# A two-layer decoder trunk on one core: its SBUF buffers laid out anew, in two stacks from the bottom and the top of a partition

## The chip, the cores and the metric

The kernel runs on one core of one Trainium2 chip. The metric is device time in microseconds (us) of one execution; three timed runs of the kernel before stand below. PE is TensorE (PEld its weight loads), DVE is VectorE, ACT is ScalarE, POOL is GpSimd, SP is SyncE, which issues the loads. Every tile lies in SBUF on 128 partitions; an address here is a byte within a partition, 0 at the bottom, 229376 at the top. All tiles of the kernel start at addresses that are fixed when the program is built.

## The reference

x is [512 tokens, 1024]. Layer 0 mixes by sparse attention and pooling, layer 1 by a convolution module; each layer ends in a feed-forward part with 2816 hidden channels.

```python
def conformer_conv(h, w_pw1, b_pw1, w_dw, b_dw, ln_g, ln_b, w_pw2, b_pw2):
    a, gt = jnp.split(h @ w_pw1 + b_pw1, 2, axis=-1)
    z = a * jax.nn.sigmoid(gt)
    z = lax.conv_general_dilated(z, w_dw[:, None, :], ..., feature_group_count=D_MODEL) + b_dw   # causal, 31 taps
    z = jax.nn.silu(layernorm(z, ln_g, ln_b))
    return z @ w_pw2 + b_pw2

def swiglu(h, w_gate, w_up, w_down):
    return (jax.nn.silu(h @ w_gate) * (h @ w_up)) @ w_down

for layer in range(2):
    h = rmsnorm(x, mix_norm[layer])
    x = x + (nsa_pool_mixer(h, ...) if layer == 0 else conformer_conv(h, ...))
    h = rmsnorm(x, ffn_norm[layer])
    x = x + swiglu(h, ffn_w_gate[layer], ffn_w_up[layer], ffn_w_down[layer])
return rmsnorm(x, final_norm)
```

## The kernel before

Channels lie on partitions, tokens in columns: the residual is 8 tiles `x0` to `x7` of 128 x 512. A product is exact to float32 in three float32r passes: both operands are split into a high and a low part, and for each of the k-tiles of the contraction TensorE runs high x high, high x low and low x high into one bank (`mm3`). The stationary operand is the split weight (`wh`, `wl`), the moving operand, 512 columns of it, the split activation.

- **Weights** come in units of 128 x 1024 (512 KB). SP loads each into one of 3 buffers `raw`; ACT writes `wh` (a copy to float32r), DVE (for some units POOL) writes `wl` = `raw` - `wh`, 3 buffers of each.
- **Norm pairs.** The residual times a norm's gain, split, stands in a ring of 8 pairs, `xs...h` and `xs...l`: `xsm0` feeds the attention's projections, `xsf0` the feed-forward part of layer 0, `xsm1` the first pointwise product of the convolution (`pa`, `pg`). The same ring holds the inputs of the attention's output product `op` (`mp`, `mo`, all but the pair `mo0`) and the convolution's results `ys` (input of the second pointwise product `p`, in halves of 256 tokens). The norm pairs of layer 1's feed-forward part, `xsf1`, stand in a ring of their own (pool `n1`, tags `xnh`, `xnl`).
- **Feed-forward part.** 22 hidden tiles in chunks of 8, 8 and 6. For each hidden tile a gate product `g` and an up product `u`, 8 k-tiles x 3 passes = 24 matmuls of 512 columns each, whose moving operands are the norm pairs; the hidden tile goes through the scratch tile `a` into a pair `hd...h`, `hd...l`. After a chunk come 8 down products `d` of 8 (or 6) x 3 matmuls, whose moving operands are the `hd` pairs, and DVE adds each to `x`. The last chunk of layer 1 runs its down products in halves of 256 columns.
- **Convolution module.** Tiles 0 to 4 are convolved by DVE, ACT and POOL from `z0` to `z4` (ACT products of one tap go to POOL by a ring of 8 buffers `pr`), tiles 5 to 7 by TensorE (`tz`, from `zp` into `zo`). Squares for the LayerNorm's variance are the tiles `lsq`.

The order of instructions on each engine is written out by a small planner inside the kernel (`run_tasks`), with its own table of costs; addresses play no part in it. Tiles get their addresses from pools, which are stacked from the bottom of a partition or, with `side="right"`, from its top, in the order in which they are opened. A ring's buffers are laid out when its first tile is made.

```python
with tc.tile_pool(name="cn", bufs=1) as cn, tc.tile_pool(name="wp", bufs=1) as wp, \
        tc.tile_pool(name="xp", bufs=1) as xp, tc.tile_pool(name="ps", bufs=1, space=PSUM) as pp:
...
    raws[i] = wp.tile([P, UW], F32, name=f"raw{i}", tag="raw", bufs=3)
```

This is where the tiles that matter lie, from the program as built:

| tiles | read by TensorE as | bytes before | bytes after the change |
|---|---|---|---|
| DMA scratch | | 0 to 16384 | 0 to 1024 |
| `raw` (3) | | 19584 to 31872 | 208736 to 221024 |
| `wh`, `wl` (3 each) | stationary; moving in `pab`, `v` | 31872 to 56448 | 4224 to 28800 |
| `x0` to `x7` | | 56448 to 72832 | 192352 to 208736 |
| `xs` ring (8 pairs) | moving | 72832 to 89216, 91264 to 107648 | 28800 to 61568 |
| `acc`, `sq`, `bc` | | 89216 to 91264, 107648 to 113920 | 221024 to 229344 |
| `hd` pairs (both layers) | moving | 120064 to 152832 | 61568 to 94336 |
| `a` (3) | | 113920 to 120064 | 94336 to 100480 |
| `xsf1` | moving | 196576 to 229344 | in the `xs` ring |
| `ys` | moving | in the `xs` ring | 61568 to 94336 |
| `z0` to `z4` | | 113920 to 124800 | 94336 to 105216 |
| `pr` (8) | | 147712 to 164096 | 77952 to 94336 |
| attention's tiles | partly | 113920 to 228416 | 61568 to 176064 |

Of the kernel before, what the change touches and what calls it, by code (L numbers as in the profile page):

```python
# [7 lines left out]
F32 = mybir.dt.float32  # L8
# [5 lines left out]
P = 128  # L14
T = 512            # tokens
D = 1024           # model width
KT = D // P        # k-tiles of the model width
TB = T // P        # token blocks
NH = 8             # heads
DH = 64  # L20
NC = 31            # compressed blocks
FH = 2816
FT = FH // P       # 22 hidden tiles
FCH = (8, 8, 6)    # hidden tiles by chunk
CW = 31            # conv taps
UW = D             # widest weight unit (columns)
# [4 lines left out]
# columns of the packed constants (shapes only)  # L31
C_ID = 0           # identity
C_ONE = 128        # ones
C_HALF = 256       # -0.5 [4]
C_REP = 260        # identity of 32, repeated [4, 32]
C_ATT = 388        # from here on only for the attention layer
C_M = 0            # token distances, masked
C_MC = 512         # distances to compressed blocks, transposed: rows [2, 32], a column per token
C_CNT = 1024       # 1 / min(t + 1, w) [4, 16]
C_Q = 1088         # query scale by pair [4]  # L40
C_RM = 1092        # tokens with a whole compressed block [1]
C_SEL = 1093       # the blocks' two halves and their positions, summed [key / value, 2, 64]
NATT = 1349

# columns of the packed vectors
V_MN = 0           # mix_norm [2, 8]
V_FN = 16          # ffn_norm [2, 8]
V_FIN = 32         # final_norm [8]
V_PS = 40          # pool_scale [4]
V_BP1 = 44         # conv_b_pw1 [16]  # L50
V_DW = 60          # conv_w_dw [8, 31]
# [4 lines left out]
V_PK = 340         # cmp_pos_k [16]  # L56
V_PV = 356         # cmp_pos_v [16]
NVEC = 372

PH = 4             # token phases that TensorE's convolution puts on the partitions  # L60
NTZ = 37 * PH      # columns of a tile's taps and bias, by phase
# the plan: times are in microseconds of the engines' clocks that run_tasks keeps; a prio is a place in TensorE's work
WINDOW = 600       # tasks that are looked at
WB = 3             # buffers of split weights
BANKS = {'A': 2, 'B': 2, 'C': 2, 'D': 2}
AHEAD = 10.5       # how long before its product a weight unit's split becomes urgent
TOL = 0            # how late a more urgent task may be and still go first, in layer 0
TOL1 = 0.1         # and in layer 1
SHARE = (0, 40)    # weight units whose low parts VectorE and GpSimd share

# layer 0
FILL = (39, 55, 72, 88, 95, 105, 114)   # where queries and pool channels are projected
I0 = 50            # the first item: a head's branch
ITEM = 7.0         # from an item to the next
LAG = 17.0         # from an item's scores to its values
# [5 lines left out]
CEARLY = 4         # items from a head pair's compressed weights to its first item  # L81
# [4 lines left out]
PBRANCH = 9       # item that the pooling goes with  # L86
SBANK = 15         # items before the scores take turns in two rings of banks
LEAD0 = 3          # output projections that start with the first inputs

# layer 1  # L90
VT = 5             # conv tiles of the other engines
PRB = 8            # products on the way from ScalarE to GpSimd
SLACK = 0        # room that GpSimd's part of a conv tile leaves
TZLAG = 1          # tiles between a gate and TensorE's convolution
MEANS = 97         # where the first half's means are taken
LATE = (4, 7)      # tiles that come after the others' mean is taken
MARGIN = 2
HIGHS = (1, 3, 5)   # tiles of the first half whose high parts ScalarE may take
LEAD = 2           # second pointwise products that start with the first results
LATE1 = 20  # L100
LNB = 122          # where the second half's norm is
PREP2 = 17         # AHEAD of the second pointwise products
# [18 lines left out]
def body(tc, I, out):  # L121
# [17 lines left out]
    class Engine:  # L139
        """An engine: its instructions stay in their order, and are timed."""  # L140
# [5 lines left out]
        def about(self, n):  # L146
            """The time of an instruction on n columns, roughly."""
            return self.cost("", n, ())
# [4 lines left out]
        def __getattr__(self, name):  # L153
            def emit(*args, **kw):
# [3 lines left out]
                parts = tile_of(out)[:2] in ("zp", "zo", "tz")        # written by parts  # L158
# [17 lines left out]
    class Products(Engine):  # L176
        """The tensor engine, whose clock follows how busy it was in the tick before."""
# [51 lines left out]
    def hop(a, b):  # L229
        """From an engine's result to another's start."""  # L230
        return b.chain if a is b else HOPS.get((a, b), 0.06)
# [3 lines left out]
    def fetch(dst, src):  # L235
        """A load, timed."""
        nc.sync.dma_start(dst, src)
        loads[0] = max(loads[0], (used.get(tile_of(dst)) or (0.0,))[0] + 1.5) + cols(dst) * P * 4 / 360e3
        wrote[tile_of(dst)] = (loads[0] + 1.0, None)

# [1 line left out]
    queue, slots, fill_from, tol = [], {}, [0.0], [TOL]  # L242

    class Task:
        """A step on an engine, or on the soonest of several; end: when it ends, once it is emitted."""
# [24 lines left out]
    class Buf:  # L270
        """A tile of a ring of buffers, made by its first task; it waits for the uses of the one before it."""
# [17 lines left out]
    def put(engines, fn, deps=(), prio=0.0, n=T, new=(), into=(), uses=(), after=(), first=False):  # L289
        """A task that calls fn with its engine when deps have ended and after has begun; the lower prio first.  # L290
        new: buffers that it writes first; into: others that it writes; uses: those that it reads."""
# [12 lines left out]
    def resolve(t):  # L304
        """When a task can start, as far as its inputs go."""
# [12 lines left out]
    def candidate(e, open_tasks):  # L318
        """An engine's next task, and when it would start."""
# [49 lines left out]
    class Timed:  # L369
        """A pool whose tiles wait, in that timing, for the ones before them in their buffers."""  # L370
# [12 lines left out]
    class Stage:  # L383
        """A pool that is opened when it is first used, after others are closed."""
# [51 lines left out]
    with tc.tile_pool(name="cn", bufs=1) as cn, tc.tile_pool(name="wp", bufs=1) as wp, \  # L436
            tc.tile_pool(name="xp", bufs=1) as xp, tc.tile_pool(name="ps", bufs=1, space=PSUM) as pp:
        cn, wp, xp, pp = (Timed(v) for v in (cn, wp, xp, pp))
# [6 lines left out]
        n1 = Stage("n1", [tzs], side="right")  # L445
        f1 = Stage("f1", [cv])
# [13 lines left out]
        def load_to(n):  # L460
            while next_load[0] < min(n, len(units)):
                i = next_load[0]
                w = units[i].shape[1]
                raws[i] = wp.tile([P, UW], F32, name=f"raw{i}", tag="raw", bufs=3)
                fetch(raws[i][:, :w], units[i])
                next_load[0] += 1

        def unit_split(i, prio):
            """The task that ends the split of a weight unit into two float32r parts."""
# [32 lines left out]
        def product(tag, u, src, name, prio, deps=(), seg=ALL, by_k=None, lead=None, ahead=AHEAD, floor=-1e9):  # L502
            """A weight unit's product with src's pairs of buffers: its task, its bank.
            by_k: what the steps wait for; lead: the steps' own prio, to start with the first inputs."""
# [29 lines left out]
        class Norm:  # L534
            """The residual, scaled by a norm's gain and split; 1/rms by token."""

            def __init__(self, tag, gcol=None, pool=xp, ring="xs"):
# [4 lines left out]
                if gcol is not None:  # L542
                    self.hs = [tuple(Buf(pool, ring + p, KT, f"xs{tag}{j}{p}", dtype=F32R) for p in "hl") for j in range(KT)]
# [3 lines left out]
            def write(self, b):  # L547
                """How a task writes one of the norm's buffers: as the first, or after others."""
# [5 lines left out]
            def tile(self, j, seg, deps, prio, late=0.0):  # L554
                """Tasks for a tile of the residual: its parts, its squares added up."""
# [15 lines left out]
            def stats(self, seg, prio, tag="D"):  # L571
                """Tasks that bring 1/rms to all partitions."""
# [12 lines left out]
        def rsqrt(name, n, sp, sums, eps, prio, tag, shift=None):  # L585
            """Per token 1/sqrt(sums / D + eps), on all partitions in a bank: the task, the bank, the values by token block.
            shift: tasks, bank and place of other sums, whose squares / D are first taken off."""
# [27 lines left out]
        def residual(j, seg, t, o, prio, bias=None):  # L615
            """A product added to a tile of the residual."""
# [8 lines left out]
        def gate_up(l, c, fp, us, nm, hid, prio, lead=0):  # L625
            """Hidden tiles of a chunk, split."""
            for i in range(FCH[c]):
# [6 lines left out]
                k = put(V, lambda e, a=a, go=go: V.tensor_tensor(a(), go(), nm.bc(), op=ALU.mult), [g, *nm.done.values()], p + 5, new=(a,), uses=(go, nm.bc))  # L634
# [487 lines left out]
        def conformer(nm, base):  # L1122
# [26 lines left out]
            class Conv:  # L1149
# [9 lines left out]
                def src(self, k):  # L1159
                    return z[self.i][:, k:k + T]  # L1160
# [433 lines left out]
```

## Time and profile before

| | before |
|---|---|
| median of 3 runs | 1222.38 us (1222.06 to 1223.82) |
| span of the profiled execution | 1220.5 us |
| TensorE busy in the span | 1145.4 us (94%), 5563 matmuls |
| mean granted clock of TensorE | 0.973 |
| VectorE, ScalarE, GpSimd busy | 706.8, 506.2, 364.6 us |
| read from HBM | 106.66 MB, 89 GB/s over the span |

The profile gives the span from the first to the last instruction; the runs' times are those of whole executions, 1.9 us more at the median. A row of the timeline is an instruction with its start and its duration; the ends of matmuls are modelled, so the pace of TensorE is read from the starts, one product's start to the next one's. In the table of windows, "x" is the number of instructions in a stretch and PEclk the granted clock, 1.00 being 2.4 GHz.

### The profile page before, as it was taken

Reading aid. Unit: us, or ns where it says so; the run is one execution under the profiler, and the core shown is the slowest. Engines: PE = TensorE matmul, PEld = TensorE weight load, DVE = VectorE, ACT = ScalarE, POOL = GpSimd, SP = SyncE. Lnnn points to the kernel's source line nnn. Section 1 sums busy time; section 2 is a strip of 40 time slices with the busy share of each in tenths; the row PEclk is TensorE's granted clock in tenths of the full one; section 3 lists DMA queues with packets and bytes.
Section 4 is the critical chain, followed back from the end, with each engine's and each line's share of the span. In section 5 each row is a group of like instructions: output and inputs, shape, how many; then the busy total and the mean of one; then the engine's idle time right before and its main releaser. Section 6 shows DMA issues by size and latency. Waiting matters only on the chain. (4 is left out here: it accounts for less than half of the span.)

```text
span 1220.5 us, 14692 instructions
## 1 busy us (share of the span) xinstructions
PE 1145.4 (94%) x5563; PEld 952.1 (78%) x5563; DVE 706.8 (58%) x1064; ACT 506.2 (41%) x833; POOL 364.6 (30%) x317
## 2 busy tenths in 40 slices
PE   7989999999999999999999646899999999999996
PEld 5868878778888888888788536788888888888895
DVE  6778996556333433344589999695443333333355
ACT  5657685333222321223476446664332223222253
POOL 1056662166101110011269864242110011101123
PEclk9989999999999999999999877899999999999998
DMA  6311112223323232322322101144223232332243
GB/s 242 115 66 35 53 35 72 100 88 103 104 86 104 86 104 88 102 90 84 104 86 83 42 14 36 48 144 137 104 86 104 87 101 90 92 98 90 87 130 109
DMA packets 34264, 110.77 MB, mean 91 GB/s; under 512 B 3856, under 2 KB 6416, under 8 KB 34192
## 3 DMA queue, kind: packets, MB, share of 16 engines
q1 hardware_dynamic: 33904, 109.56, 28.0%
q8 instruction: 44, 0.72, 0.3%
q14 instruction: 28, 0.23, 0.1%
q10 hardware_dynamic: 288, 0.26, 0.1%
HBM read 106.66 MB, written 2.10 MB: 89 GB/s over the span
## 5 line engine op out<-in xcount | busy, mean ns | idle before, releaser
L155 ACT ACTIVATE wh<-raw 128x1024 fp32r<-128x1024 f32 (+4 forms) x205 | 209.2, 1025 | 532.5 <-PE d L155 161.9
L155 DVE TENSOR_TENSOR wl<-raw,wh 128x1024 fp32r<-128x1024 f32 (+3 forms) x193 | 240.4, 1248 | 35.9 <-ACT wh L155 32.5
L155 POOL TENSOR_TENSOR a<-a,bcf 128x512 f32<-128x512 f32 x44 | 78.4, 1783 | 541.1 <-ACT a L155 541.1
L155 POOL TENSOR_TENSOR cl<-cl,pr 128x512 f32<-128x512 f32 x69 | 99.4, 1443 | 48.2 <-ACT pr L155 43.5
L155 DVE TENSOR_TENSOR a<-u,a 128x512 f32<-128x512 f32 x44 | 30.4, 691 | 137.1 <-PE u L155 130.7
L155 DVE TENSOR_TENSOR x<-d,x 128x512 f32<-128x512 f32 (+1 forms) x56 | 34.3, 614 | 127.0 <-PE d L155 127.0
L155 DVE TENSOR_TENSOR a<-g,bcf 128x512 f32<-128x512 f32 x44 | 30.4, 691 | 122.4 <-PE g L155 115.9
L155 PE MATMUL tz<-zp,tz 128*128 128x128 f32 x216 | 32.0, 319 | 29.4 <-DVE zo L155 16.5
L155 PEld LDWEIGHTS tz<-zp,tz 128*128 128x128 f32 x216 | 31.3, 234 | 31.1 <-issue 19.8
L155 ACT ACTIVATE pr<-z,vec 128x512 f32<-128x512 f32 x69 | 46.7, 714 | 18.8 <-POOL cl L155 18.7
L155 DVE SCALAR_TENSOR_TENSOR cp<-z,vec,cp 128x512 f32<-128x512 f32 x75 | 54.0, 750 | 0.8
L155 POOL TENSOR_TENSOR p<-p,rc 128x512 f32<-128x512 f32 (+1 forms) x64 | 50.0, 802 | 2.4
L155 ACT ACTIVATE p<-s,mn 128x512 f32<-128x512 f32 (+1 forms) x64 | 33.3, 525 | 21.6 <-DVE mn L155 18.0
L155 DVE COPY zp<-ta 32x128 f32<-32x128 f32 x36 | 35.7, 992 | 0.6
L155 DVE CUSTOM_DVE_ANT_0 s<-s,att 128x512 f32<-128x512 f32 (+1 forms) x64 | 30.7, 503 | 8.4 <-PE s L155 8.2
L155 POOL TENSOR_TENSOR wl<-raw,wh 128x1024 fp32r<-128x1024 f32 (+1 forms) x12 | 29.5, 2469 | 17.4 <-ACT wh L155 17.3
L155 DVE TENSOR_TENSOR l<-tp,h 128x512 fp32r<-128x512 f32 (+1 forms) x48 | 27.9, 592 | 6.4 <-ACT h L155 6.2
L155 POOL TENSOR_TENSOR tz<-con,vph 128x1152 f32<-128x1152 f32 x12 | 30.0, 2526 | 0.0
L155 ACT ACTIVATE h<-tp 128x512 fp32r<-128x512 f32 (+1 forms) x48 | 24.4, 524 | 11.8 <-PE tp L155 11.1
L155 ACT ACTIVATE a<-a 128x512 f32<-128x512 f32 x44 | 27.2, 618 | 1.4 <-DVE a L155 1.3
L155 PE MATMUL s<-kh,qs 128*128 128x512 f32 (+1 forms) x64 | 21.7, 343 | 4.8 <-ACT p L155 4.8
L155 PE MATMUL tp<-con,p 128*128 128x128 f32 x160 | 24.0, 275 | 2.0 <-DVE l L155 2.0
(1326 smaller groups left out, 3425.1 us busy)
## 6 DMA issues: line engine op xcount, KB each, us to landing
raw<-in_w_gu SPq DMA_DIRECT2D x88, 512.0 KB, 3.5
raw<-in_w_dn SPq DMA_DIRECT2D x32, 512.0 KB, 3.5
raw<-in_w_p SPq DMA_DIRECT2D x32, 512.0 KB, 3.5
raw<-in_w_dn SPq DMA_DIRECT2D x24, 384.0 KB, 3.0
raw<-in_w_in SPq DMA_DIRECT2D x12, 512.0 KB, 4.0
raw<-in_w_out SPq DMA_DIRECT2D x8, 512.0 KB, 3.4
x<-in_x SPq DMA_DIRECT2D x8, 256.0 KB, 6.3
raw<-in_w_c SPq DMA_DIRECT2D x4, 512.0 KB, 3.8
```

Of the source, the lines that this page charges most:

```text
L155: tc.keep_in_program_order(getattr(self.eng, name)(*args, **kw))
```

## The change

Pools are opened in another order and on other sides. The split weights stand alone at the bottom, above them a new pool with the norm pairs; `raw`, `x`, `acc`, `sq` and `bc` move to the top. The ring of layer 1's own norm pairs goes, and `xsf1` takes the common ring. To make that free, the convolution's results `ys` get a ring `yh` and the ring `pr` in the convolution's pool, both made first; the squares of the second half's LayerNorm then take the rings `ta` and `tg` in place of `pr`. In the feed-forward pools the `hd` rings are made ahead of `a`. `zo` is made before `zp`, and the `z` tiles have 32 columns of padding ahead in place of 30. The scratch of the DMA queues shrinks. The comments and docstrings go too. Its code, but for those:

```diff
-    with tc.tile_pool(name="cn", bufs=1) as cn, tc.tile_pool(name="wp", bufs=1) as wp, \
-            tc.tile_pool(name="xp", bufs=1) as xp, tc.tile_pool(name="ps", bufs=1, space=PSUM) as pp:
+    with tc.tile_pool(name="cn", bufs=1) as cn, tc.tile_pool(name="wp", bufs=1) as wp, \
+            tc.tile_pool(name="xs", bufs=1) as xsp, tc.tile_pool(name="xp", bufs=1, side="right") as xp, \
+            tc.tile_pool(name="ps", bufs=1, space=PSUM) as pp:
...
-        n1 = Stage("n1", [tzs], side="right")
-        f1 = Stage("f1", [cv])
+        f1 = Stage("f1", [cv, tzs])
...
-                raws[i] = wp.tile([P, UW], F32, name=f"raw{i}", tag="raw", bufs=3)
+                raws[i] = xp.tile([P, UW], F32, name=f"raw{i}", tag="raw", bufs=3)
...
-                    self.hs = [tuple(Buf(pool, ring + p, KT, f"xs{tag}{j}{p}", dtype=F32R) for p in "hl") for j in range(KT)]
+                    self.hs = [tuple(Buf(xsp, "xs" + p, KT, f"xs{tag}{j}{p}", dtype=F32R) for p in "hl") for j in range(KT)]
...
+                def scaled(e, a=a, go=go, h=h, lo=lo, first=i == c == 0):
+                    if first:
+                        h(), lo()
+                    V.tensor_tensor(a(), go(), nm.bc(), op=ALU.mult)
...
+            yx = [(Buf(cv, "yh", KT, f"ys{i}h", dtype=F32R), Buf(cv, "pr", PRB, f"ys{i}l", dtype=F32R)) for i in range(KT)]
...
             def make_inputs(e):
+                for h, _ in yx:
+                    h()
+                G.memset(cv().tile([P, T], F32, name="pr", tag="pr", bufs=PRB)[:, 0:1], 0.0)
                 for i in range(KT):
                     if i < VT:
-                        z[i] = cv().tile([P, CW - 1 + T], F32, name=f"z{i}")
-                        G.memset(z[i][:, 0:CW - 1], 0.0)
+                        z[i] = cv().tile([P, ZP + T], F32, name=f"z{i}")
+                        G.memset(z[i][:, 0:ZP], 0.0)
...
-                    q = Buf(cv, "pr", PRB, f"lsq{hf}{i}") if hf else Buf(cv, "tg", 2, f"lsq{hf}{i}")
+                    q = Buf(cv, "ta", 1, "lsq10") if hf and not i else Buf(cv, "tg", 2, f"lsq{hf}{i}")
...
-                    if hf == 0:
-                        yx[i] = tuple(Buf(xp, "xs" + k, KT, f"ys{i}{k}", dtype=F32R) for k in "hl")
...
-            nm1 = Norm("f1", V_FN + KT, n1, "xn")
+            nm1 = Norm("f1", V_FN + KT)
...
-    nc = _bacc.Bacc("TRN2", target_bir_lowering=False, num_devices=1)
+    nc = _bacc.Bacc("TRN2", target_bir_lowering=False, num_devices=1, dynamic_dma_scratch_size=1024)
```

As built, PE, DVE, ACT and SP issue the same instructions in the same order as before; POOL issues one more. This is POOL's program at the start of the convolution module, of the kernel before; `z0` to `z4` are the padded inputs of the convolution.

```order
L155 TENSOR_TENSOR rm10_4987<-vm10_4985,con_67 128x4 [waits DVE_49]
L155 MEMSET z0_5017 128x30 [waits PE_49]
L155 MEMSET z1_5019 128x30
L155 MEMSET z2_5021 128x30
L155 MEMSET z3_5023 128x30
L155 MEMSET z4_5025 128x30
L155 MEMSET zp5_5027 128x4x8
```

And the same place after the change:

```order
L156 TENSOR_TENSOR rm10_4990<-vm10_4988,con_70 128x4 [waits DVE_49]
L156 MEMSET pr_5028 128x1 [waits PE_49]
L156 MEMSET z0_5030 128x32
L156 MEMSET z1_5032 128x32
L156 MEMSET z2_5034 128x32
L156 MEMSET z3_5036 128x32
L156 MEMSET z4_5038 128x32
L156 MEMSET zp5_5041 128x4x8
```

The added memset takes the first one's place and its wait for TensorE (the last down product of layer 0, whose `hd` tiles lay there). The second place is ACT's program at the LayerNorm of the second half of the tokens, where `lsq1i` is the square of tile i; before:

```order
L155 ACTIVATE lsq10_6243<-z0_5017 128x256 [waits DVE_49,Pool_49]
L155 ACTIVATE lsq11_6249<-z1_5019 128x256 [waits DVE_49,Pool_49]
L155 ACTIVATE lsq12_6255<-z2_5021 128x256 [waits DVE_49,Pool_49]
L155 ACTIVATE wh116_6262<-raw116_6064 128x1024 [waits DMAHW0_49,PE_49,Pool_49]
L155 ACTIVATE wh117_6276<-raw117_6091 128x1024 [waits DMAHW1_49,PE_49,Pool_49]
L155 ACTIVATE lsq13_6291<-z3_5023 128x256 [waits DVE_49]
L155 ACTIVATE lsq14_6296<-z4_5025 128x256 [waits DVE_49]
```

After:

```order
L156 ACTIVATE lsq10_6248<-z0_5030 128x256 [waits DVE_49]
L156 ACTIVATE lsq11_6254<-z1_5032 128x256 [waits DVE_49,PE_49]
L156 ACTIVATE lsq12_6260<-z2_5034 128x256 [waits DVE_49,PE_49]
L156 ACTIVATE wh116_6267<-raw116_6077 128x1024 [waits DMAHW0_49,PE_49,Pool_49]
L156 ACTIVATE wh117_6281<-raw117_6104 128x1024 [waits DMAHW1_49,PE_49,Pool_49]
L156 ACTIVATE lsq13_6296<-z3_5036 128x256 [waits DVE_49,Pool_49]
L156 ACTIVATE lsq14_6301<-z4_5038 128x256 [waits DVE_49,Pool_49]
```

The instructions stand as they stood. From `lsq13` on, each now waits until POOL has added the square two places before it, since its ring has two buffers in place of eight.

## Rows read from the trace of the kernel before

**Rows 1.** The page: busy time, share of the span and instructions of each engine.

```profile
PE 1145.4 (94%) x5563; PEld 952.1 (78%) x5563; DVE 706.8 (58%) x1064; ACT 506.2 (41%) x833; POOL 364.6 (30%) x317
```

**Rows 2.** The table of windows, all instructions; columns as in its first line.

```profile
core 0: us, PE busy (x) PEld busy (x) DVE busy (x) ACT busy (x) POOL busy (x), PEclk, DMA share, GB/s
400.00:500.00 100.00, 100.00 (x438) 81.79 (x437) 38.10 (x42) 24.98 (x29) 9.26 (x6) 1.00 0.31 96
700.00:800.00 100.00, 70.02 (x423) 63.97 (x423) 85.63 (x157) 56.45 (x105) 41.27 (x31) 0.80 0.14 45
1000.00:1100.00 100.00, 100.00 (x431) 80.72 (x430) 38.12 (x42) 25.03 (x29) 9.04 (x5) 1.00 0.30 95
```

**Rows 3.** The timeline of PE, layer 0: first matmul of a product g, u, d, g, u.

```profile
402.17 0.39 PE L155 MATMUL g<-xsf00h,wh 128*128 128x512 f32 x1
...
407.61 0.39 PE L155 MATMUL u<-xsf00h,wh 128*128 128x512 f32 x1
...
456.57 0.40 PE L155 MATMUL d<-hd010h,wh 128*128 128x512 f32 x1
...
501.36 0.39 PE L155 MATMUL g<-xsf00h,wh 128*128 128x512 f32 x1
...
506.81 0.39 PE L155 MATMUL u<-xsf00h,wh 128*128 128x512 f32 x1
```

**Rows 4.** The chain that ended last, in order of time: start, us, what, matmuls.

```profile
829.26 4.31 PE p L155 x36
...
912.83 5.60 PE g L155 x24
918.43 5.60 PE u L155 x24
924.03 44.62 PE d L155 x192
...
1058.25 44.62 PE d L155 x192
...
1172.41 17.94 PE d L155 x149
```

**Rows 5.** The timeline of PE in layer 1: matmuls of one up product.

```profile
918.50 0.39 PE L155 MATMUL u<-xsf10l,wh 128*128 128x512 f32 x1
918.73 0.40 PE L155 MATMUL u<-xsf10h,wl 128*128 128x512 f32 x1
918.97 0.39 PE L155 MATMUL u<-xsf11h,wh 128*128 128x512 f32 x1
919.20 0.39 PE L155 MATMUL u<-xsf11l,wh 128*128 128x512 f32 x1
```

**Rows 6.** The tile `raw` between 400 and 470: duration ns least/median/most, times.

```profile
L155 ACT ACTIVATE wh<-raw x13: 1061/1061/1064, 402.2 to 467.8; 128x1024 fp32r<-128x1024 f32 x13
L155 DVE TENSOR_TENSOR wl<-raw,wh x13: 1224/1225/1226, 403.3 to 468.9; 128x1024 fp32r<-128x1024 f32 x13
...
DMA to landing us min/median/max: 3.4/3.5/4.4
```

**Rows 7.** The timeline of PE, the attention's output product: first matmul of two products.

```profile
217.48 0.39 PE L155 MATMUL op<-mp0h,wh 128*128 128x512 f32 x1
...
222.97 0.39 PE L155 MATMUL op<-mp0h,wh 128*128 128x512 f32 x1
```

**Rows 8.** The timeline of POOL and of ACT, the second half's squares and the memsets.

```profile
606.70 0.35 POOL L155 MEMSET z<- 128x30 f32 x5
...
785.93 1.55 POOL L155 TENSOR_TENSOR lsq<-lsq,lsq 128x256 f32<-128x256 f32 x2 [3.35 <-ACT lsq L155]
788.89 4.28 POOL L155 TENSOR_TENSOR lsq<-lsq,lsq 128x256 f32<-128x256 f32 x3 [1.40 <-ACT lsq L155]
...
788.35 0.71 ACT L155 ACTIVATE lsq<-z 128x256 f32<-128x256 f32 x2
...
790.65 0.42 ACT L155 ACTIVATE lsq<-zo 128x256 f32<-128x256 f32 x1
```

**Rows 9.** The timeline of PE in the attention, moving operands from `wh` and `wl`.

```profile
39.60 0.28 PE L155 MATMUL pab<-wh,c2l 128*128 128x256 f32 x1
...
40.67 0.28 PE L155 MATMUL pab<-wh,c2l 128*128 128x256 f32 x1
...
48.86 0.29 PE L155 MATMUL v<-wh,xsm03h 128*128 128x280 f32 x1
48.99 0.30 PE L155 MATMUL v<-wl,xsm03h 128*128 128x280 f32 x1
...
49.65 0.29 PE L155 MATMUL v<-wh,xsm05h 128*128 128x280 f32 x1
49.78 0.29 PE L155 MATMUL v<-wl,xsm05h 128*128 128x280 f32 x1
```

More of the change, by code (lines that the diff above doesn't have):

```diff
@@ L58 @@
 NVEC = 372
+ZP = 32
 PH = 4
@@ L436, in body @@
     with tc.tile_pool(name="cn", bufs=1) as cn, tc.tile_pool(name="wp", bufs=1) as wp, \
-            tc.tile_pool(name="xp", bufs=1) as xp, tc.tile_pool(name="ps", bufs=1, space=PSUM) as pp:
-        cn, wp, xp, pp = (Timed(v) for v in (cn, wp, xp, pp))
+            tc.tile_pool(name="xs", bufs=1) as xsp, tc.tile_pool(name="xp", bufs=1, side="right") as xp, \
+            tc.tile_pool(name="ps", bufs=1, space=PSUM) as pp:
+        cn, wp, xsp, xp, pp = (Timed(v) for v in (cn, wp, xsp, xp, pp))
         at = Stage("at")
@@ L534, in body, with __init__ @@
         class Norm:
-            def __init__(self, tag, gcol=None, pool=xp, ring="xs"):
+            def __init__(self, tag, gcol=None):
                 self.tag, self.gcol = tag, gcol
@@ L633, in gate_up @@
                 g, go = product("A", us[i][0], nm.hs, "g" + t, p, lead=step)
-                k = put(V, lambda e, a=a, go=go: V.tensor_tensor(a(), go(), nm.bc(), op=ALU.mult), [g, *nm.done.values()], p + 5, new=(a,), uses=(go, nm.bc))
+                def scaled(e, a=a, go=go, h=h, lo=lo, first=i == c == 0):
+                    if first:
+                        h(), lo()
+                    V.tensor_tensor(a(), go(), nm.bc(), op=ALU.mult)
+                k = put(V, scaled, [g, *nm.done.values()], p + 5, new=(a,), uses=(go, nm.bc))
                 k = put(S, lambda e, a=a: S.activation(a(), a(), AF.Silu), [k], p + 5, uses=(a,))
@@ L1069, in pooled @@
                 uses_of[u_pool].append(t)
-                h, lo = mixed[i] = tuple(Buf(xp, "xs" + p, KT, f"mp{i}{p}", dtype=F32R) for p in "hl")
+                h, lo = mixed[i] = tuple(Buf(xsp, "xs" + p, KT, f"mp{i}{p}", dtype=F32R) for p in "hl")
                 sc = vec[:, V_PS + i:V_PS + i + 1]
@@ L1079, in head_out @@
                 if s == 0:
-                    mixed[4 + pr] = tuple(Buf(xp if pr else at, ("xs" if pr else "mo") + p, KT if pr else 1, f"mo{pr}{p}", dtype=F32R) for p in "hl")
+                    mixed[4 + pr] = tuple(Buf(xsp if pr else at, ("xs" if pr else "mo") + p, KT if pr else 1, f"mo{pr}{p}", dtype=F32R) for p in "hl")
                     outs[pr] = [Buf(ap, tag, 1, f"{tag}{pr}") for tag in ("om", "ol")], []
@@ L1134, in zc @@
             def zc(i, seg):
-                v = z[i][:, CW - 1:] if i < VT else zo[i]
+                v = z[i][:, ZP:] if i < VT else zo[i]
                 return v[:, seg]
             def make_inputs(e):
+                for h, _ in yx:
+                    h()
+                G.memset(cv().tile([P, T], F32, name="pr", tag="pr", bufs=PRB)[:, 0:1], 0.0)
                 for i in range(KT):
                     if i < VT:
-                        z[i] = cv().tile([P, CW - 1 + T], F32, name=f"z{i}")
-                        G.memset(z[i][:, 0:CW - 1], 0.0)
+                        z[i] = cv().tile([P, ZP + T], F32, name=f"z{i}")
+                        G.memset(z[i][:, 0:ZP], 0.0)
                     else:
+                        zo[i] = cv().tile([P, T], F32, name=f"zo{i}")
                         zp[i] = cv().tile([P, PH, 8 + T // PH], F32, name=f"zp{i}")
-                        zo[i] = cv().tile([P, T], F32, name=f"zo{i}")
                         G.memset(zp[i][:, :, 0:8], 0.0)
@@ L1159, in src @@
                 def src(self, k):
-                    return z[self.i][:, k:k + T]
+                    return z[self.i][:, ZP - CW + 1 + k:ZP - CW + 1 + k + T]
                 def vector(self):
@@ L1253, in gated @@
                 def gated(e):
-                    o = z[i][:, CW - 1:] if i < VT else ta()
+                    o = z[i][:, ZP:] if i < VT else ta()
                     V.scalar_tensor_tensor(o, ta(), vec[:, V_BP1 + i:V_BP1 + i + 1], tg(), op0=ALU.add, op1=ALU.mult)
@@ L1339, in conformer @@
             after_sums = []
-            yx, bl = {}, Buf(cv, "bl", 1, "bl")
+            bl = Buf(cv, "bl", 1, "bl")
             def layer_norm(hf, p0):
@@ L1419, in conformer @@
             yt.append(layer_norm(1, base + LNB))
-            nm1 = Norm("f1", V_FN + KT, n1, "xn")
-            ysrc = [yx[i] for i in range(KT)]
+            nm1 = Norm("f1", V_FN + KT)
             for hf, seg in enumerate(HALF):
@@ L1426, in conformer @@
                     p = base + PW0 + PWH * hf + PWS * j
-                    t, o = product(P2T[hf][j % len(P2T[hf])], u_p2[hf][j], ysrc, f"p2{hf}{j}", p, seg=seg, by_k=yt[hf],
+                    t, o = product(P2T[hf][j % len(P2T[hf])], u_p2[hf][j], yx, f"p2{hf}{j}", p, seg=seg, by_k=yt[hf],
                                    lead=base + PWL + j * 0.01 if hf == 0 and j < LEAD else None, ahead=PREP2, floor=base + FLOOR)
@@ L1498, in body @@
             raise KeyError(E.t)
-        for s in (f1, n1):
-            s.close()
+        f1.close()
 def _constants():
```

## The prediction

> **What bounds the kernel now.** I read the page first [rows 1]: TensorE is busy for 1145.4 of 1220.5 us, the next engine for 58%. The average hides the stages, so the table of windows comes next [rows 2]. The reader is to see two kinds of stretch. In the feed-forward parts (400 to 500 in layer 0, 1000 to 1100 in layer 1) TensorE is busy for 100.00 of 100 us at granted clock 1.00, the others for 9 to 38%: time is matmuls times pace, and nothing else ends last there. In the convolution module (700 to 800) TensorE is down to 70.02 at a clock of 0.80, and DVE at 85.63 leads.
>
> Third, the count of matmuls in the two full windows: 438 in layer 0, 431 in layer 1. Both are saturated, with the same kinds of products, the same clock, the same DMA share (0.31, 0.30) and DVE and ACT busy alike. So layer 1 runs at another pace. The timeline and the chain say where. In layer 0 a product of 24 matmuls takes 407.61 - 402.17 = 5.44 us, 226.7 ns a matmul, and a chunk of down products 501.36 - 456.57 = 44.79 us for 192, 233.3 ns [rows 3]. In layer 1 g and u take 5.60 us, 233.3 ns, and a chunk of d 44.62, 232.4 ns [rows 4]. 512 columns at 2.4 GHz are 213.3 ns; all four are over that, one by 13.3 ns and three by 19 to 20.
>
> What is the same in g of both layers: weights (same buffers), banks, engines beside them, instruction. What differs is the place of the moving operand. The table of addresses in the section on the kernel puts the quick one at 72832 to 107648, the slow ones at 120064 to 152832 (`hd`) and 196576 to 229344 (`xsf1`). Misalignment isn't it alone: `hd` starts at a multiple of 128 bytes as `xs` does. Two readings fit. Either a moving operand below some address between 107648 and 120064 streams at the better pace, or it does when its start and the weights' start are alike modulo 512 bytes (72832 and 31872 both leave 128; `hd` leaves 256, `xsf1` 480). I can't tell them apart here, and needn't: after the change `wh`, `wl`, `xs`, `hd` and `ys` all lie below 94336 and all leave 128.
>
> **The change part by part.**
>
> *Gate and up products of layer 1.* 22 hidden tiles, so 44 products, from 5.60 to 5.44 us: 44 x 0.16 = **-7.0 us** [rows 3, 4]. Bounds: 0 if the pace stays. The floor of the row is 5.44; nothing shows a quicker product.
>
> *Down products of layer 0.* A chunk of 192 at 226.7 ns would take 43.52 us in place of 44.79: -1.27. There are 192 + 192 + 144 = 528 matmuls, 2.75 such chunks: **-3.5 us** [rows 3].
>
> *Down products of layer 1.* Two chunks of 512 columns at 44.62 [rows 4]: 2 x (44.62 - 43.52) = **-2.2 us**.
>
> *Last chunk of layer 1, and p.* These stream 256 columns. The slow place gives 17.94 us for 149 down matmuls, 120.4 ns, the quick one 4.31 for 36 of p, 119.7 [rows 4]. So the place is worth next to nothing at 256 columns: 288 x 0.7 ns = 0.2 us, taken as **0**, bounds -0.2 and +0.2.
>
> *Output product of the attention.* Of its eight pairs only `mo0` lies high; a product takes 222.97 - 217.48 = 5.49 us [rows 7], 0.05 over the quick pace, and `mo0` moves only from above 166000 to about 107552. 8 x 0.05 = 0.4 is the bound; I take **0**, since I can't place the threshold.
>
> *What covers TensorE's neighbours.* A quicker product asks for a weight unit each 5.44 us. ACT's `wh` takes 1.06, DVE's `wl` 1.23, the load lands in 3.5 (4.4 at most) with three buffers [rows 6], and layer 0 already keeps that pace with TensorE full. No new wait in the feed-forward parts.
>
> *Padding, memset, rings.* The memset of one column joins five that take 0.35 us together [rows 8] behind the same wait; below 0.1 us, and it is long before the convolution's first input. The squares from `lsq13` on now wait for POOL's add two places back. ACT does `lsq13` and `lsq14` from 788.35; the adds for which they wait end with the pair at 785.93 + 1.55 = 787.48. `lsq15` at 790.65 waits for the first of three that take 4.28 from 788.89, so about 1.43 us for one: 790.32 [rows 8]. Nothing is late by these rows; the margin of 0.33 us is thin, and a loss of up to 0.3 is the bound. Queued behind it on ACT are norm parts of layer 1 and `wh` copies, and DVE and TensorE's p products wait for those.
>
> *Other moves.* `x`, `raw`, `acc` and `bc` change places only for DVE, ACT, POOL and the loads. Instructions of one shape on those engines show no difference by address in this trace where they meet no neighbour, so 0; bounds -0.5 and +1, the latter for the convolution module, where DVE leads [rows 2].
>
> **Sum:** -7.0 - 3.5 - 2.2 = -12.7 us, on the span 1220.5 - 12.7 = 1207.8. The runs' median stands 1.9 us above the span, so I forecast 1222.4 - 12.7 = **1209.7 us**. By its bounds the case goes from 1206.5 (the 0.2, 0.4 and 0.5 above, and some of the attention's scores whose operands come lower, which I put at 2 at most) to 1213 (a pace between the two on one of the three terms).
>
> The Trainium skill, "TensorE: Matmul & The Clock Gate", section "Back-to-back issue gap", gives an isolated gap of N / 2.4 + 2.5 ns, with no word of where the operand lies; "SBUF — State Buffer", section "Who interferes with whom", says that PE never waits on another engine. By these the layout would be worth nothing and the time stay at 1222 (rival A). The gap by that formula, 215.8 ns at 512, isn't met by either layer: the rows have 226.7 and 233.3, so here the trace carries more weight.
>
> **The rivals.**
>
> *A. No change, about 1222.* The difference between the layers would come from something that stays: the order of loads, or a state of the chip late in the program. For it: in both layers one thing besides the place differs, the time. Against it: in layer 0 the pace goes from 226.7 to 233.3 at the first `hd` and back at the next g (506.81 - 501.36 = 5.45 us) [rows 3], within one chunk, and the only thing that turns with it is the moving operand. In layer 1, where both operands lie high, g and d are both slow [rows 4].
>
> *B. Slower, about 1229: the lowest addresses are slow too.* The quick pace is only seen from 72832 on. No 512-column moving operand of before lies under it, and `xs` goes to 28800 to 61568. The nearest rows are `v` and `pab`, which stream `wh` and `wl` from 31872 to 56448 [rows 9]. `pab` does 9 in 40.67 - 39.60 = 1.07 us, 118.9 ns, as 256 columns do anywhere. `v` does six of 280 columns in 49.65 - 48.86 = 0.79, 131.7 ns, 15 over its 116.7, and with uneven steps (130 to 140 ns) as the slow place shows them [rows 5] (230 to 240 ns). If that is the slow pace, the 44 products of layer 0 lose 44 x 0.16 = 7.0 us, `pa` and `pg` (384 matmuls x 6.6 ns) 2.5, the attention's own projections and output product (480) 3.2; layer 1's g and u stay at 5.60; `hd` at 61568 still gains 5.7. Sum +7.0: 1229. It decides if 512 columns from below 61568 take over 230 ns. Against it: `v`'s pieces begin at odd offsets, which alone could make the steps uneven, and its excess of 15 ns is nearer to the 13.3 of the quick place than to the 20 of the slow one.
>
> *C. Half of it, about 1215.* Only `xsf1`, off by 96 bytes from a multiple of 128, is cured by the move (-7.0), and the gain on `hd` does not come. Against it: `hd` is slow while aligned [rows 3].
>
> **How the numbers follow.** My forecast gets 0.66, C 0.08, A 0.11, B 0.15. Of runs within 0.2% (2.4 us) I say "same", since a measurement of this kernel tells no less: 0.11. Faster is the forecast and C, 0.74; slower is B, 0.15. The predicted time is the forecast's, 1209.7. For 8 in 10 the range starts at 1206.5 and must take in C and A: up to 1223. B lies outside. The likeliest case alone is 1206.5 to 1213.
>
> **What would show it.** In the changed kernel's chain, g and u of layer 1 at 5.44 us for 24, its d at about 43.5 for 192; in layer 0's timeline, d at 43.5 per chunk and g unchanged at 5.44; a full window of layer 1 with some 440 matmuls in place of 431. Wrong: g of layer 0 at 5.6 (B), g of layer 1 still at 5.60 (A), d above 44.5 (C). An add of `lsq` that ACT waits for would show as idle time before `lsq15` named after POOL.

## The result, and the profile after

The changed kernel takes 1208.82 us (median of 4 runs, 1208.26 to 1210.15), the kernel before 1222.52 beside it: ratio 0.9893, 95% interval 0.9879 to 0.9907. The profiled execution's span fell from 1220.5 to 1206.9 us.

The page of the changed kernel, busy time of each engine as in [rows 1]:

```profile
PE 1132.4 (94%) x5563; PEld 951.3 (79%) x5563; DVE 707.4 (59%) x1064; ACT 506.7 (42%) x833; POOL 365.1 (30%) x318
```

13.0 us have gone from TensorE's busy time with the same 5563 matmuls; VectorE, ScalarE and GpSimd are as busy as before, within 0.6 us each. Its table of windows, for the stretches of [rows 2]:

```profile
400.00:500.00 100.00, 100.00 (x443) 82.83 (x442) 38.84 (x44) 26.08 (x30) 9.09 (x5) 1.00 0.32 98
700.00:800.00 100.00, 71.15 (x442) 65.57 (x441) 86.60 (x157) 59.89 (x113) 44.91 (x35) 0.80 0.14 47
1000.00:1100.00 100.00, 100.00 (x443) 82.84 (x442) 38.18 (x42) 24.48 (x28) 10.89 (x6) 1.00 0.31 95
```

A full window now holds 443 matmuls in either layer, where it held 438 and 431, at the same granted clock of 1.00. The chain of the changed kernel, as in [rows 4], shows which products became quicker:

```profile
455.54 43.52 PE d L156 x192
499.06 5.44 PE g L156 x24
...
824.52 4.32 PE p L156 x36
...
895.11 5.44 PE g L156 x24
900.55 5.44 PE u L156 x24
...
916.87 43.52 PE d L156 x192
...
1047.43 43.52 PE d L156 x192
...
1158.59 18.14 PE d L156 x149
```

The gate and up products of layer 1 went from 5.60 to 5.44 us, the down products of 512 columns from 44.79 and 44.62 to 43.52 for 192. The products of 256 columns gained nothing: `p` went from 4.31 to 4.32, and the 149 `d` at the end from 17.94 to 18.14. One wait that the prediction put a bound on did come. In the timeline of ACT, the second half's squares:

```profile
786.34 0.42 ACT L156 ACTIVATE lsq<-zo 128x256 f32<-128x256 f32 x1
788.01 0.42 ACT L156 ACTIVATE lsq<-zo 128x256 f32<-128x256 f32 x1 [0.45 <-POOL lsq L156]
790.51 0.40 ACT L156 ACTIVATE lsq<-zo 128x256 f32<-128x256 f32 x1
```

ACT idles 0.45 us ahead of `lsq16` for POOL's add, which is the ring of two buffers at work. In the kernel before it idled there as well, for VectorE:

```profile
792.12 0.42 ACT L155 ACTIVATE lsq<-zo 128x256 f32<-128x256 f32 x1 [0.25 <-DVE zo L155]
```

So the ring adds 0.2 us to a wait that was there.

### The profile page after: what moved, and what is told of

The parts are those of the page before. It is cut to its first block, busy times and chain, and to the rows that moved or that the text cites. A ratio compares the mean times of both kernels' runs of the same rounds, so it can differ in the third digit from the quotient of the medians.

```text
span 1206.9 us, 14696 instructions
## 1 busy us (share of the span) xinstructions
PE 1132.4 (94%) x5563; PEld 951.3 (79%) x5563; DVE 707.4 (59%) x1064; ACT 506.7 (42%) x833; POOL 365.1 (30%) x318
## 4 chain that ended last, share of the span: by engine, by line
PE 76%; DVE 13%; POOL 4%; issue 3%; ACT 2%; DMA 0%; DVEq 0%; SPq 0%; POOLq 0%; ACTq 0%
PE u L156 21%; PE d L156 20%; PE g L156 20%; PE op L156 3%; DVE zp L156 3%; DVE cp L156 3%; PE p L156 2%; POOL cl L156 2%; DVE wl L156 1%; PE o L156 1%; PE s L156 1%; PE q L156 1%; PE v L156 1%; PE tp L156 1%; PE pa L156 1%
```

## The experiments

The prediction left two readings of the quick pace open: a place low in the partition, or starts of moving operand and weights that are alike modulo 512 bytes. A third is that the moving operand's own start decides. "Difference" below is the moving operand's start minus the weights' start, modulo 512. It is 0 for the `xs` ring before and for all the tiles in question after; before it was 128 for `hd` and 352 for `xsf1`.

**Pads in the kernel before (k1_before_pads).** The old layout stays whole, and nothing moves by more than 384 bytes.

```diff
+PAD = {"f0": 384, "f1": 384}
...
+                if self.name in PAD:
+                    self.pool.tile([P, PAD[self.name] // 4], F32, name="pad" + self.name)
...
+            if tag == "xnl" and len(ring) == 1:
+                self.pool.tile([P, 88], F32, name="padn1")
```

> The kernel before with three pads and nothing else: 384 bytes ahead of a and hd in both feed-forward pools (hd from 120064 to 120448) and 352 bytes behind layer 1's own norm pairs (from 196576 to 196224). Both now leave 128 modulo 512, as wh, wl and the xs ring do, and both stay high in the partition. Place theory (a moving operand below some address near 112000 is quick): no pace changes, 1222.4 us. Relation theory (quick when the moving operand's start and the weights' start are alike modulo 512) and own-start theory (quick when the moving operand's own start leaves 128 modulo 512): g and u of layer 1 go to 5.44 us, a chunk of d to 43.5, in all -12.7, about 1209.7 us.

Measured: 1208.91 us, ratio 0.9897 (0.9876 to 0.9917). Its chain:

```profile
909.75 5.44 PE u L156 x24
915.19 43.52 PE d L156 x192
```

The place theory falls: with `hd` at 120448 and `xsf1` at 196224 the paces are those of the changed kernel, and so is the time. Three pads are enough for all that the change gained; the two stacks, the moved residual and raw weights and the smaller scratch add nothing that these runs can tell.

**128 bytes ahead of the moving operands (k2_moving_128).**

```diff
+        xsp.tile([P, 32], F32, name="pad")
```

> The changed kernel with 128 bytes ahead of the norm pairs, so that all moving operands above (xs, hd, ys) leave 256 modulo 512, while wh and wl still leave 128. Place theory: nothing changes, 1208.8 us. Relation and own-start theories: every product of 512 columns goes to 5.60 us for 24; some 3900 such matmuls by 6.6 ns are +25, about 1234 us.

Measured: 1225.25 us, ratio 1.0027 (1.0018 to 1.0037), slower than the kernel before. Its chain:

```profile
619.65 5.60 PE pa L156 x24
...
923.00 5.57 PE u L156 x24
928.58 44.61 PE d L156 x192
```

So 128 bytes cost 16 us, though the norm pairs, `hd` and `ys` still lie at the bottom. The expected +25 was too much, for two reasons: the pace came out at 5.57 to 5.59 us and not at 5.60, and the sum counted products of the attention and of the convolution module as if they lay on the path. The `pa` product does go to 5.60 us here, but from the first `pa` matmul to the LayerNorm's sums `rest` the timeline has 166.7 us, against 166.4 in the changed kernel. The feed-forward products explain the span: 88 x (5.575 - 5.44) = 11.9, 4.75 chunks of d by 1.1 = 5.2, together 17.1 of the 17.5 us (1224.4 - 1206.9).

**128 bytes ahead of everything (k3_both_128).**

```diff
+        cn.tile([P, 32], F32, name="pad")
```

> The changed kernel with 128 bytes at the very bottom, so that weights and moving operands all leave 256 modulo 512. Place theory: 1208.8 us. Relation theory: nothing changes either, 1208.8. Own-start theory: all products of 512 columns slow, about 1234 us.

Measured: 1210.43 us, ratio 0.99 (0.9877 to 0.9923). Its chain:

```profile
909.14 5.44 PE u L156 x24
914.58 43.52 PE d L156 x192
```

Moving operands and weights both leave 256 now, and all is quick: the moving operand's own start does not decide.

**128 bytes ahead of the weights (k4_weights_128).**

```diff
+        wp.tile([P, 32], F32, name="padw")
+        xsp.tile([P, 96], F32, name="padx")
```

> The changed kernel with 128 bytes ahead of wh and wl, which then leave 256 modulo 512, and 384 ahead of the norm pairs, whose starts and those of hd and ys again leave 128. Place theory: 1208.8 us. Relation theory: all products of 512 columns at 5.60, about 1234 us. Own-start theory: no change, 1208.8 us.

Measured: 1226.12 us, ratio 1.0032 (1.002 to 1.0044). Its chain:

```profile
921.02 5.60 PE u L156 x24
926.62 44.80 PE d L156 x192
```

The moving operands start modulo 512 where they do in the changed kernel, and only the weights have shifted; these products of layer 1 are as slow as before (in layer 0 they take 5.57 to 5.59 us). The time again misses the expected 1234, whose sum counted the same products off the path. Of the three theories only the relation has held through all four kernels.

**Which differences are quick.** Three kernels, one run each, with pads ahead of the norm pairs and of the `hd` rings of either layer (the first is shown):

```diff
+PADX = 256
+PAD = {"f0": 320, "f1": 192}
...
+        xsp.tile([P, PADX // 4], F32, name="padx")
```

> The changed kernel with pads so that (moving start minus weights' start) modulo 512 is 256 for the norm pairs, 64 for layer 0's hd and 448 for layer 1's. If only a difference of 0 is quick: g and u at 5.58 to 5.60 us for 24, d at 44.6 to 44.8 for 192, about 1225 us. If the modulus is 256: g and u at 5.44, d slow, about 1214 us. A difference with a pace under 5.44 would show here too, if there is one.

> As the run with 256, 64 and 448, with differences of 32 for the norm pairs, 96 for layer 0's hd and 192 for layer 1's. If only 0 is quick: all slow, about 1225 us. If nearness to 0 counts, g and u at a difference of 32 lie between 5.44 and 5.60.

> As the run with 256, 64 and 448, with differences of 320 for the norm pairs, 160 for layer 0's hd and 480 for layer 1's. If only 0 is quick: all slow, about 1225 us; 480 is 32 short of 512 and shows nearness from the other side.

Measured: 1210.15, 1227.9 and 1220.78 us. The chain of the kernel with 256, 64 and 448:

```profile
323.81 43.96 PE d L158 x192
...
911.58 5.44 PE u L158 x24
917.02 44.80 PE d L158 x192
```

Of the kernel with 32, 96 and 192:

```profile
922.90 5.60 PE u L158 x24
928.50 44.80 PE d L158 x192
```

Of the kernel with 320, 160 and 480:

```profile
502.53 5.60 PE g L158 x24
...
919.72 5.49 PE u L158 x24
925.21 44.79 PE d L158 x192
```

A difference of 256 is as quick as 0, against "only 0" (a g right behind a slow chunk of d aside, 5.46 or 5.49 us). 64 and 320 can lie between: 5.49 us for a product in layer 1 at 320, and 43.96 for a chunk of layer 0's d at 64 in the first of the three. All others tried (32, 96, 128, 160, 192, 352, 384, 448, 480) take 5.57 to 5.60 a product, or 44.6 to 45.0 a chunk. For 512 columns the modulus is thus 256, and being near to 0 counts for nothing: 32 is as slow as 96. But away from 0 and 256 the difference alone does not fix the pace. At 320 the twelve g and u of layer 0's last chunk take 5.60 us in the same run, and those of its first two chunks 5.49; why stays open.

**Differences under 32 bytes (k10_16_8_bytes).**

```diff
+    class Off(Buf):
+        def __init__(self, pool, tag, bufs, name, off):
+            super().__init__(pool, tag, bufs, name, (P, T + P), F32R)
+            self.off = off
+        def __call__(self):
+            return super().__call__()[:, self.off:self.off + T]
```

> The changed kernel with layer 0's hidden tiles 16 bytes and layer 1's 8 bytes into wider buffers of 2560 bytes, so that the difference is 16 and 8 modulo 512; the norm pairs keep 0. If any difference but 0 (or 256) is slow: a chunk of d 44.6 to 44.8 us in both layers, about 1214 us. If steps under 32 bytes don't count: 43.5 and 1208.8. If a small difference is quicker than 0: under 43.5.

Measured: 1213.52 us. Layer 0's chunks of d at 16 bytes take 44.48 us, and layer 1's at 8 bytes 44.81, beside g and u that keep a difference of 0:

```profile
323.16 44.48 PE d L157 x192
...
913.05 5.44 PE u L157 x24
918.49 44.81 PE d L157 x192
```

Eight bytes are enough to lose the pace, and neither 8, 16 nor 32 beats 0.

**The low weights alone (k8_wl_apart).**

```diff
+                    if i == 0:
+                        wp.tile([P, 32], F32, name="padl")
...
+        xsp.tile([P, 96], F32, name="padx")
```

> The changed kernel with 128 bytes between wh and wl alone: wl leaves 256 modulo 512, wh and all moving operands 128. One matmul in three has its own weights off, and one in three streams while weights that are off come next. If the relation acts matmul by matmul: 24 take about 5.49 us (8 of them slow by 6.6 ns), about 1214 us. If one odd pair upsets those around it: 5.58 and more, about 1225 us. Place or own-start theory: 1208.8 us. In the timeline, the step that is longer tells whether it is the matmul with wl as its own weights, or the one ahead of it.

Measured: 1224.48 us. Its chain, and its timeline of PE within one up product:

```profile
888.30 5.55 PE u L156 x24
893.85 5.55 PE g L156 x24
```

```profile
925.58 0.39 PE L156 MATMUL u<-xsf16h,wh 128*128 128x512 f32 x1
925.81 0.40 PE L156 MATMUL u<-xsf16l,wh 128*128 128x512 f32 x1
926.04 0.40 PE L156 MATMUL u<-xsf16h,wl 128*128 128x512 f32 x1
926.28 0.39 PE L156 MATMUL u<-xsf17h,wh 128*128 128x512 f32 x1
926.50 0.40 PE L156 MATMUL u<-xsf17l,wh 128*128 128x512 f32 x1
```

The steps from 925.81 are 0.23, 0.24 and 0.22: l x `wh` with `wl` next, h x `wl` with `wh` next, h x `wh` with `wh` next. Averaged over the g products of layer 1 the three are 232.5, 234.1 and 226.7 ns from the timeline's starts. Two in three are slow, where one or all had been expected: 5.44 + 16 x 0.0066 = 5.55, as measured. So a matmul is quick when both its own weights and the weights that come next agree with its moving operand. Whether the next weights count against the moving operand or against the weights ahead of them, this run can't tell, since `wh` and the moving operands start alike in it.

**Products of 256 columns (k9_256_quick, k11_last_chunk).** In the sweep the last down products went to 17.18 us for 149 at differences of 448 and 192, from 18.14 at 0. The row at 448:

```profile
1161.34 17.18 PE d L158 x149
```

Two kernels shift products of 256 columns alone; the first is shown.

```diff
+PAD = {"cv": 448}
...
+            if tag == "heh" and (id(self), tag) not in rings:
+                self.pool.tile([P, 112], F32, name="padhe")
...
+            if l == 1 and c == len(FCH) - 1:
+                return [tuple(Buf(fp, "he" + p, FCH[c], f"hd{l}{c}{i}{p}", dtype=F32R) for p in "hl") for i in range(FCH[c])]
```

(the second kernel without the pad in `cv`)

> The changed kernel with two more shifts, for the products of 256 columns alone: the convolution's results ys start 448 bytes later (64 modulo 512, a difference of 448 to the weights), and the last chunk's hidden tiles of layer 1 get rings of their own at the same difference; all products of 512 columns keep a difference of 0. By the sweep, 256 columns take about 272 cycles there in place of 288. If the steps count on the path: 288 down matmuls by 6.5 ns are -1.9 us and the 192 p matmuls of the second half -1.2, about 1205.7 us. If the weights' split or the adds on VectorE set the end of these stretches: no change from 1208.8.

> The changed kernel with the last chunk's own rings alone (difference 448 for 288 down matmuls of 256 columns), ys left at a difference of 0: -1.9 us if the steps count, about 1206.9 us; no change if other engines set the end there.

Measured: 1206.47 us, ratio 0.988 (0.9864 to 0.9897), and 1207.56, ratio 0.9886 (0.9871 to 0.9901). Chain of the second:

```profile
824.30 4.32 PE p L156 x36
...
1158.40 17.18 PE d L156 x149
```

And of the first:

```profile
822.01 4.24 PE p L157 x36
...
1156.19 17.81 PE d L157 x149
```

Both medians lie under the changed kernel's, but the intervals overlap its 0.9879 to 0.9907, so that they beat it is not shown. The stretches say a little more. From the first `d` of the last chunk to the end the timelines have 50.85 us in the changed kernel, 49.03 in the second kernel, near the -1.9 that was expected, and 49.88 in the first. The first kernel's span (1203.5 us) is 3.4 us under the changed kernel's, but 1.7 of these lie in the attention, ahead of the first g, where the two have the same addresses. With the same difference of 448, the last `d` takes 17.18 us in two kernels and 17.81 in the third. So at 256 columns the difference alone does not fix the pace; what else does stays open.

## Why the prediction was right, and where it was not

- **What bounds it, and the pace by the moving operand's layout:** right. The feed-forward parts were TensorE's matmuls times pace, and the pace is what changed.
- **Gate and up products of layer 1, -7.0:** 44 x (5.60 - 5.44), as forecast; the chain has 5.44 after.
- **Down products of layer 0, -3.5, and of layer 1, -2.2:** 43.52 for a chunk, the very figure of the sum.
- **256 columns, 0:** right in size, with the sign the other way. The forecast compared the last `d` with `p`, two different products, and expected the better layout to be quicker by 0.2 us at most; it is slower by 0.2. That is no accident of one run: the last `d` takes 18.14 us in all three kernels with a difference of 0 (the changed one, k1 and k3), and 17.94 or 17.95 at 128 and 384 (the one before, k2 and k4). The last experiments show that the pace there can be moved further, which the forecast did not see.
- **The two readings left open:** the first, an address between 107648 and 120064, is wrong; the second, starts alike modulo 512, is right but for the modulus, which is 256 for 512 columns.
- **The squares' ring:** the wait fell ahead of `lsq16`, where I had named `lsq15` and a bound of 0.3. I had split the 4.28 us of the three adds evenly and looked at the first alone. In the trace of the kernel before the second add starts at 790.57 and takes 1.77 us, so it ends 0.2 us after the 792.12 at which `lsq16` began: the wait could have been read there. From `lsq15` to the first `p` of the second half the timelines have 14.70 us after, 14.53 before, and 14.52 in the kernel before with three pads, which keeps the ring of eight; so the ring cost about 0.2 us, inside the bound. The stretch from there to the first g of layer 1 was not longer (27.6 us after, 28.2 before).
- **Output product of the attention:** the pair `mo0` came down to 107552 and 113696 and its product still takes 5.47 us, against 5.49 [rows 7]. By the relation that fits, since its start leaves 32 modulo 512 and the weights' 128.
- **Sum:** the span was forecast at 1207.8 and is 1206.9. By the timelines the three terms came to -12.6, as summed: from layer 0's first g to the first `pa` 366.3 us became 362.8 (-3.5), and from layer 1's first g to the first `d` of its last chunk 336.5 became 327.4 (-9.1, forecast -9.2). The end of the program took 0.2 us more and the attention 0.1 more. What the forecast did not have is -1.3 us from the first `pa` to layer 1's first g (233.2 before, 231.9 after), most of it (167.2 to 166.4) ahead of the LayerNorm's sums `rest`. This may be scatter, since runs of the kernel before alone lie between 1222.06 and 1223.82; the kernel before with three pads, whose convolution tiles lie in their old places, has 232.2 there. No run tells what else it might be.

**The rivals.** *B* (the lowest addresses are slow) fell with `xs` at 28800 and 5.44 us. The uneven `v` of [rows 9], which spoke for it, is not explained by the relation: its 280 columns take 129.8 ns in the pieces whose operands start alike, 132.0 in those with a difference of 96 and 126.9 in those with 192, by the starts in the trace before and the program's addresses. So the rule found here is one for 512 columns. *A* (no change) fell: 128 bytes cost 16 us. The rule of the Trainium skill on which A leaned ("SBUF — State Buffer", section "Who interferes with whom": PE never waits on another engine) isn't contradicted by that, since what counts here is the place of PE's own two operands, and A took more from it than it says. *C* fell: `hd`, aligned to 128 bytes, did gain.

## What to carry to other kernels

When the same product runs at two paces in one program with the clock, the neighbours and the banks alike, compare the starts of the operands in SBUF, modulo a few hundred bytes, before looking for a wait. In this kernel a product of 512 float32r columns kept its best pace when the moving operand and all the weights of its neighbourhood started at the same place modulo 256 bytes; a pad of a few hundred bytes did all the work of the new layout. A layout that is moved for another reason should be looked at for this too: an added constant or a padding column ahead of the tiles can cost 1.4% (1225.25 us against 1208.82).

## What the runs showed of the hardware that was not expected

- Back-to-back float32r matmuls of 512 columns at granted clock 1.00 take 226.7 ns each (5.44 us for 24) when the differences of the starts are 0 or 256 modulo 512, and 232 to 234 ns at most others; 8 bytes are enough (233.4 ns, 44.81 us for 192). Away from 0 and 256 one difference can have two paces: at 320, 5.49 and 5.60 us for 24 in the same run. High or low in the partition made no difference in these runs.
- The effect acts matmul by matmul, and the weights that come next count as well as a matmul's own: with `wl` shifted alone, two of three steps are slow (232.5, 234.1, 226.7 ns).
- At 256 columns the order is another: 149 of the last down products' matmuls take 18.14 us at a difference of 0, 17.18 at 448 in two kernels, and 17.81 in a third with the same difference.
